# Attention heads by halves of the PE array, experts chosen by counting, a dummy pow, and scratch in a ring of 24 tiles

## The chip, the cores and the metric

The kernel runs on one core of a Trainium2 chip. The metric is the device time of one execution in microseconds (us), the median over several executions. The core has five engines with queues of their own: PE (matrix products; its weight loads are listed as PEld), DVE and ACT (element by element), POOL (rarely used here) and SP, which only issues transfers from DRAM.

## The reference

Two layers over 256 tokens of width 1024. Layer 0 mixes tokens with a gated convolution and stick-breaking attention, layer 1 with a gated MLP. Each layer then has a mixture of 32 experts (4 groups of 8; top group, then its top 2) and a gated embedding. All weights are float32, 257 MB in all.

```python
def even_mixer(xn, w_in, conv_w, w_out):
    proj = xn @ w_in
    ...
    y_a = short_conv_mixer(h, gb, gc, conv_w)
    y_b = stick_breaking_attention(q.reshape(shp), k.reshape(shp), v.reshape(shp))
    y = jnp.concatenate([y_a, y_b.reshape(B, S, SB_WIDTH)], axis=-1)
    return y @ w_out
...
def hier_moe(xn, wc, bc, wf, bf, w1, w3, w2):
    pc = jax.nn.softmax((xt @ wc + bc).astype(jnp.float32), axis=-1)
    pg, gi = lax.top_k(pc, 1)
    ...
    pf = jax.nn.softmax(lf_sel, axis=-1)
    wtop, ei = lax.top_k(pf, TOP_K)
    ...
    for e in range(N_EXPERTS):
        he = jax.nn.silu(xt @ w1[e]) * (xt @ w3[e])
        y = y + comb[:, e:e + 1] * (he @ w2[e])
```

## The kernel before

**Weights.** Nearly all weights come as tiles of 1 MB (128 partitions x 2048 float32), one transfer each, issued by SP in `emit_loads` (L109), in the order in which they are used. They land in a ring of 23 places (`rawp`, BUFS); a new tile takes the place that was released longest ago, and its transfer waits for the last user of that place. A tile of the dense stages is split into a high part `wh` (ACT, L126) and the rest `wl` (DVE, L136), each again a place of the ring, and each product is made of three (`mm3`). Expert tiles are used as they are. Some intermediate tensors (`att`, `xc`, `hT`, `o`) take places too; others have buffers of their own (`act`).

**How far ahead.** `emit_loads` goes on as long as `len(raws) + 2 * len(done) + 1 + SPARE + hold <= BUFS`, where `raws` are the tiles loaded and not yet split or used, `done` the split ones, SPARE is 4 and `hold` a number that each stage sets: HOLD[0] at the start, HOLD[1] after the attention, HOLD[3] when the odd mixer's output loop begins, HOLD[4] late in that loop, HOLD[2] after an expert stage, MOE_HOLD[0] (-2) in `finish_mixer`, which ends each mixer, and the other MOE_HOLDs inside the expert stage.

**Layer 0.** The input projection goes in column blocks (`proj_cols`, PE L411). For each of the two halves of the heads, `att_z` makes the scores z of two pairs of heads (a pair is 128 rows: head i in rows 64 i to 64 i + 63), then come softplus work on ACT and DVE and two or three projection blocks, `att_sum` (the running sum, PE L600 and L603) and `att_av` (the products with v, L612 and L613). `finish_mixer` makes the last output product, the router's logits (`lps`, L468) and 40 matmuls that have no use but to keep PE busy (L495).

**Expert stage.** The router (L786 to L820) picks the group by `first_max` and two experts in it by two more, each a chain of a maximum, an equality with a descending ramp `desc`, another maximum and another equality. The mask Mb goes to PE (L826), which counts positions; `gather` (L855) brings the tokens of a group together, and the 8 rounds q do `up` (hps, L907) with w1 and w3, and `down` (yps, L960) with w2; the 32-column quarters of the array each have another expert. The first users of the preloaded tiles are the first hps.

**The setup** has POOL make index ramps (jp first), from which DVE makes the identity and the masks; PE warms up for some us and transposes rows and x. `rstd` (POOL L370) is a power of -0.5.

**Layer 1** is as layer 0 with the gated MLP: `proj_u`, `gate`, and an output loop of 8 rounds.

## Time and profile before

| | us |
|---|---|
| median of 3 runs | 770.53 (766.19 to 770.72) |
| profiled execution | 771.92 |
| its span, first to last instruction | 770.1 |
| PE busy | 674.0 (88%) |
| DVE busy | 329.5 (43%) |
| ACT busy | 235.6 (31%) |
| POOL busy | 23.8 (3%) |
| bytes read from DRAM | 257.28 MB |

The mean granted clock of PE is 0.952 of full speed. In the program's order the stages are: layer 0's mixer up to about 131 us, its experts to 340, embedding and the mixer of layer 1 to 522, its experts to 731, the end. A window's row gives the busy time of each engine in a stretch with its count of instructions, then the granted clock, the share of the DMA engines and the GB/s. A timeline's row gives start, duration, engine, line, operation, result<-operands, partitions x elements, and the count when neighbours are drawn together; what stands in brackets is idle time before it and what ended that.

### The profile page before, as it was taken

How to read it: one execution, taken by the hardware profiler on the slowest of the kernel's cores; microseconds unless marked ns; L12 is line 12 of the kernel's file. 1: busy time of each engine (PE TensorE's matmuls, PEld its weight loads, DVE VectorE, ACT ScalarE, POOL GpSimd, SP SyncE). 2: the span in 40 equal slices, each digit the busy share in tenths (PEclk: the TensorE clock that was granted, in tenths of full speed). 3: DMA queues.
4: the chain of work that ended last, by engine and by line, in shares of the span. 5: the costliest groups of instructions: out<-in, count | busy, mean ns of one | idle time of the engine just before them, and what ended most of it. 6: DMA issues, size and time to landing. Idle time of an engine off the chain costs nothing.

```text
span 770.1 us, 12423 instructions
## 1 busy us (share of the span) xinstructions
PE 674.0 (88%) x5268; PEld 484.5 (63%) x5268; DVE 329.5 (43%) x556; ACT 235.6 (31%) x342; POOL 23.8 (3%) x36
## 2 busy tenths in 40 slices
PE   7999999889787797689999999998989868786696
PEld 6989988745353453237788999887554525443265
DVE  6546763332233031137765866644132421311266
ACT  6425644111101201127654443524101021010074
POOL 3200000000000000001100000000000000000000
PEclk9999999899998999999999999998999989898899
DMA  9950499699999999999854745398999999999941
GB/s 313 373 199 32 167 407 428 277 425 426 427 426 426 426 426 427 424 415 409 282 182 146 273 165 193 142 419 346 417 426 425 427 426 426 426 427 423 422 161 54
DMA packets 61163, 259.18 MB, mean 337 GB/s; under 512 B 4308, under 2 KB 22896, under 8 KB 36272
## 3 DMA queue, kind: packets, MB, share of 16 engines
q1 hardware_dynamic: 60032, 255.87, 82.5%
q0 software_dynamic: 1072, 2.47, 0.9%
q8 instruction: 43, 0.70, 0.3%
q14 instruction: 16, 0.13, 0.0%
HBM read 257.28 MB, written 1.05 MB: 335 GB/s over the span
## 4 chain that ended last, share of the span: by engine, by line
PE 47%; DMA 41%; DVE 6%; ACT 2%; issue 1%; POOL 1%; SPq 0%; POOLq 0%; ACTq 0%; DVEq 0%
DMA raw<-in_moe_w_dram 36%; PE pc L411 13%; PE ops L254 9%; PE pr L254 8%; PE hps L907 6%; PE gat L855 4%; DMA raw<-in_w_pe_dram 3%; PE yps L960 1%; DMA raw<-in_w_pg_dram 1%; DVE wl L133 1%; PE gps L712 1%; PE lps L468 1%; DVE wl L136 1%; DMA h<-in_x_dram 1%; PE tp L376 1%
## 5 line engine op out<-in xcount | busy, mean ns | idle before, releaser
L907 PE MATMUL hps<-raw,xg 128*32 128x256 f32 x2048 | 151.8, 423 | 41.0 <-DMA raw<-in_moe_w_dram 33.4
L907 PEld LDWEIGHTS hps<-raw,xg 128*32 128x32 f32 x2048 | 73.9, 121 | 117.2 <-DMA raw<-in_moe_w_dram 45.5
L136 DVE TENSOR_TENSOR wl<-raw,wh 128x2048 fp32r<-128x2048 f32 (+1 forms) x45 | 95.2, 2146 | 13.4 <-ACT wh L126 13.0
L960 PE MATMUL yps<-raw,gHL 128*32 128x512 f32 x512 | 62.4, 608 | 19.8 <-ACT gHL L947 17.8
L126 ACT CAST wh<-raw 128x2048 fp32r<-128x2048 f32 (+1 forms) x41 | 73.5, 1825 | 6.5 <-DMA raw<-in_w_in_even_dram 6.5
L928 ACT CAST ST<-sl 128x256 fp32r<-128x256 f32 x16 | 6.0, 372 | 217.2 <-DVE gjunk L924 215.2
L855 PE MATMUL gat<-S,xc 128*128 128x256 f32 (+1 forms) x320 | 64.6, 367 | 8.8 <-DVE S L841 8.8
L855 PEld LDWEIGHTS gat<-S,xc 128*128 128x128 f32 x320 | 56.3, 214 | 17.6 <-DVE S L841 9.7
L971 DVE SCALAR_TENSOR_TENSOR o<-yps,gts,o 128x512 fp32r<-128x512 f32 x28 | 21.0, 750 | 94.0 <-ACT o L970 94.0
L960 PEld LDWEIGHTS yps<-raw,gHL 128*32 128x32 f32 x512 | 15.7, 111 | 55.1 <-issue 30.0
L411 PE MATMUL pc<-xTH,wh 128*128 128x256 f32 x288 | 43.1, 296 | 1.2 <-DVE wh L128 1.2
L857 DVE TENSOR_TENSOR xg<-gat,gffn 128x512 f32<-128x512 f32 x32 | 22.1, 692 | 46.3 <-PE gat L855 42.6
L254 PE MATMUL pr<-wh,xTH 128*128 128x512 f32 (+1 forms) x152 | 40.6, 389 | 1.3 <-ACT xTH L388 1.3
L411 PEld LDWEIGHTS pc<-xTH,wh 128*128 128x128 f32 x288 | 39.7, 202 | 2.0 <-ACT xTH L521 1.4
L411 PE MATMUL pc<-xTL,wh 128*128 128x256 f32 x288 | 40.5, 284 | 0.0
L970 ACT ACTIVATE o<-yps,gts 128x512 fp32r<-128x512 f32 x28 | 19.2, 687 | 69.2 <-PE yps L960 49.7
L411 PE MATMUL pc<-xTH,wl 128*128 128x256 f32 x288 | 40.3, 283 | 0.0
L254 PE MATMUL pr<-wl,xTH 128*128 128x512 f32 (+1 forms) x152 | 39.5, 381 | 0.2 <-DVE wl L136 0.2
L254 PE MATMUL pr<-wh,xTL 128*128 128x512 f32 (+1 forms) x152 | 39.1, 379 | 0.0
L448 DVE TENSOR_TENSOR h<-h,sc 128x512 f32<-128x512 f32 x56 | 36.0, 683 | 7.0 <-PE sc L979 6.5
L938 DVE TENSOR_TENSOR he<-sl,hps 128x256 f32<-128x256 f32 x16 | 6.7, 421 | 72.0 <-PE hps L907 72.0
L411 PEld LDWEIGHTS pc<-xTL,wh 128*128 128x128 f32 x288 | 37.4, 194 | 0.0
(230 smaller groups left out, 867.9 us busy)
## 6 DMA issues: line engine op xcount, KB each, us to landing
raw<-in_moe_w_dram SPq DMA_DIRECT2D x192, 1024.0 KB, 19.5
raw<-in_w_in_odd_dram SPq DMA_DIRECT2D x16, 1024.0 KB, 13.2
raw<-in_w_in_even_dram SPq DMA_DIRECT2D x11, 1024.0 KB, 11.7
raw<-in_w_pg_dram SPq DMA_DIRECT2D x8, 1024.0 KB, 15.2
raw<-in_w_out_odd_dram SPq DMA_DIRECT2D x8, 1024.0 KB, 4.9
raw<-in_w_out_even_dram SPq DMA_DIRECT2D x4, 1024.0 KB, 5.0
raw<-in_w_pe_dram SPq DMA_DIRECT2D x2, 1024.0 KB, 19.5
h<-in_x_dram SPq DMA_DIRECT2D x2, 512.0 KB, 4.8
```

The source lines that it names most:

```text
L126: nc.scalar.copy(wh[:, c], raw[:, c])
L133: nc.vector.scalar_tensor_tensor(wl[:, c], raw[:, c], cols[:, col + j:col + j + 1], f(wh[:, c]), op0=ALU.mult, op1=ALU.subtract)
L136: nc.vector.tensor_tensor(wl[:, c], raw[:, c], f(wh[:, c]), op=ALU.subtract)
L254: nc.tensor.matmul(ps, x, w, start=start and i == 0, stop=stop and i == 3 * n - 1)
L411: nc.tensor.matmul(o, w, xx, start=st, stop=True if first else i % (3 * KD) == 3 * KD - 1, skip_group_check=first)
L448: nc.vector.tensor_tensor(h[:, tt, c], h[:, tt, c], ps, op=ALU.add)
L855: nc.tensor.matmul(ps[:, k], xc[:, tt, k0 + k, :], S[g][:, tt, c0:c1], start=(tt == 0), stop=(tt == 1))
L857: nc.vector.tensor_tensor(xg[g][:, k0:k0 + n, c0:c1], ps, gffn[:, li, k0:k0 + n].unsqueeze(2).to_broadcast([P, n, m]), op=ALU.mult)
L907: nc.tensor.matmul(ps[e * CAP:(e + 1) * CAP, :], x[:, k, c:c + CAP], ts[e][:, k, :], start=(k == 0), stop=(k == KD - 1))
L960: nc.tensor.matmul(ps[s, c], gs[:, j, s], ts[e][:, j, c], start=(j == 0), stop=(j == 1))
L970: nc.scalar.activation(o[:, 0, c], ps[:, c], AF.Copy, scale=gt[:, 0:1])
L971: nc.vector.scalar_tensor_tensor(o[:, 1, c], ps[:, c], gt[:, 0:1], f(o[:, 0, c]), op0=ALU.mult, op1=ALU.subtract)
```

## The change

The ring has 24 places; the holds are adjusted. The scratch tensors `u`, `gt`, `hs`, `zc`, `yH`/`yL` of the odd mixer, `xt`, `ptok` and `gts` move from buffers of their own into the ring (`carve` cuts one place into several views). In `att_z` the products of both heads of a pair stand next to each other and the masks follow; in `att_av` head i writes columns 64 i to 64 i + 63 of the array's output, so that one cast and one subtraction do for both. The router ranks the entries by counting those that are larger, and the maxima that the gates need are made after the first gather. A power of one is computed at POOL's head and not used.

```diff
-BUFS = 23
+BUFS = 24
 SPARE = 4
-HOLD = (9, 2, 8, 5, 3)
-MOE_HOLD = (-2, 2, 8, 4, -1)
+HOLD = (10, 2, 9, 9, 6)
+MOE_HOLD = (-2, 3, 8, 4, -1)
...
+    pone = small("pone", [P, 1])
+    nc.vector.memset(pone, 1.0)
+    nc.gpsimd.tensor_tensor(pone, pone, mhalf[:, 0:1], op=ALU.pow)
     jp = act("jp", [P, P])
...
         def att_z(hp):
             z = pp.tile([P, 2, 512], F32, name="z", tag="y")
+            rows = [slice(i * 64, (i + 1) * 64) for i in range(2)]
+
+            for i, rr in enumerate(rows):
+                nc.tensor.matmul(z[:, i, 0:256], qk[rr, 1, hp, 0:P], qk[rr, 0, hp, :], start=True,
+                                 stop=True)
+            for i, rr in enumerate(rows):
+                nc.tensor.matmul(z[:, i, 256:384], qk[rr, 1, hp, P:T], qk[rr, 0, hp, P:T],
+                                 start=False, stop=True, skip_group_check=True)
             for i in range(2):
...
+                for c in (0, 256):
+                    nc.tensor.matmul(z[:, i, c:c + P], ident_b, negmask, start=False, stop=True,
+                                     skip_group_check=True)
...
+            yb = psum("yb", "tp")[:, 0:T]
+
+            for tt, c in ((0, slice(0, T)), (1, slice(P, T))):
+                for i in range(2):
+                    vs = slice(hp * P + i * 64, hp * P + (i + 1) * 64)
+                    nc.tensor.matmul(yb[i * 64:(i + 1) * 64, c], v[:, tt, vs],
+                                     aT[:, i, c.start + 128 * tt:c.stop + 128 * tt],
+                                     start=(tt == 0), stop=True, skip_group_check=tt == 1)
+            nc.scalar.copy(yH[:, 4 + hp, :], yb)
+            nc.vector.tensor_tensor(yL[:, 4 + hp, :], yb, f(yH[:, 4 + hp, :]), op=ALU.subtract)
...
-            acc = act("hs", [P, 2, T])
...
-            hs = act("hs", [P, 2, T])
+            hs, zc, acc = [halves(a) for a in carve("conv", 2 * T, 2 * T + 4, 2 * T)]
...
-            u = act("u", [P, 2, T])
+            u, gt = [a.rearrange("p (c t) -> p c t", c=2) for a in carve("u", 2 * T, 2 * T)]
...
+        def rank_in(vals, n, tagp):
+
+            d = small(tagp + "d", [P, 2, n, n])
+            nc.vector.tensor_tensor(d, vals.unsqueeze(2).to_broadcast([P, 2, n, n]),
+                                    vals.unsqueeze(3).to_broadcast([P, 2, n, n]), op=ALU.subtract)
+            nc.vector.tensor_tensor(d, d, thr[:, 0:n, 0:n].unsqueeze(1).to_broadcast([P, 2, n, n]),
+                                    op=ALU.is_gt)
+            rk = small(tagp + "r", [P, 2, n])
+            nc.vector.tensor_reduce(rk, d, axis=AX.X, op=ALU.add)
+            return rk
```

On PE, the first scores of a pair of heads in layer 0, before (head 0, then head 1, of the first pair):

```order
L567 MATMUL z<-qk 128x256
L568 MATMUL z<-qk 128x128
L570 LDWEIGHTS ident_b
L570 MATMUL z<-negmask,ident_b 128x128
L572 LDWEIGHTS ident_b
L572 MATMUL z<-negmask,ident_b 128x128
L567 MATMUL z<-qk 128x256
L568 MATMUL z<-qk 128x128
```

and after the change:

```order
L576 MATMUL z<-qk 128x256 x2
L579 MATMUL z<-qk 128x128 x2
L583 LDWEIGHTS ident_b
L583 MATMUL z<-negmask,ident_b 128x128
L583 LDWEIGHTS ident_b
L583 MATMUL z<-negmask,ident_b 128x128
L583 LDWEIGHTS ident_b
L583 MATMUL z<-negmask,ident_b 128x128
L583 LDWEIGHTS ident_b
L583 MATMUL z<-negmask,ident_b 128x128
```

The two products of 64 rows with the same number of columns are neighbours now (x2: one per head), and the four mask products come in one block.

On DVE, the router of layer 0 from the logits lg to the mask Mb, before (c: group, f1 and f2: first and second expert):

```order
L804 SCALAR_TENSOR_TENSOR lg<-lps,rstd,br_231 128x36 x2
L786 TENSOR_REDUCE cm<-lg 128x2
L789 SCALAR_TENSOR_TENSOR ce<-lg,cm,desc 128x4 x2
L792 TENSOR_REDUCE cf<-ce 128x2
L794 TENSOR_TENSOR co<-ce,cf 128x8
L810 TENSOR_TENSOR pr<-lg,co 128x64
...
L792 TENSOR_REDUCE f2f<-f2e 128x2
L794 TENSOR_TENSOR f2o<-f2e,f2f 128x16
L818 TENSOR_TENSOR f1o<-f1o,f2o 128x16
L820 TENSOR_TENSOR Mb<-f1o,co 128x64
```

and after:

```order
L812 SCALAR_TENSOR_TENSOR lg<-lps,rstd,br_235 128x36 x2
L797 TENSOR_TENSOR cd<-lg 128x32
L799 TENSOR_TENSOR cd<-cd,thr 128x32
L802 TENSOR_REDUCE cr<-cd 128x8
L817 TENSOR_SCALAR G<-cr 128x8
L819 TENSOR_TENSOR pr<-lg,G 128x64
L822 TENSOR_REDUCE lsel<-pr 128x16
L797 TENSOR_TENSOR fd<-lsel 128x128
L799 TENSOR_TENSOR fd<-fd,thr 128x128
L802 TENSOR_REDUCE fr<-fd 128x16
L826 SCALAR_TENSOR_TENSOR Mb<-fr,G 128x32 x2
```

The chain from lg to Mb has 20 instructions behind the two of lg before, and 11 after.

On SP, the end of the transfers issued ahead of the expert stages. A tile's number counts all tiles of the program in the order in which they are made, so that a leap in it shows the code that stands between. MoE 0 before, then after:

```order
L109 DMA raw_1144<-in_moe_w2_dram 128x2048
L109 DMA raw_1146<-in_moe_w3_dram 128x2048
L109 DMA raw_1148<-in_moe_w3_dram 128x2048
L109 DMA raw_1150<-in_moe_w3_dram 128x2048
L109 DMA raw_1198<-in_moe_w3_dram 128x2048
L109 DMA raw_1200<-in_moe_w1_dram 128x2048
L109 DMA raw_1412<-in_moe_w1_dram 128x2048
```

```order
L113 DMA raw_1138<-in_moe_w3_dram 128x2048
L113 DMA raw_1140<-in_moe_w3_dram 128x2048
L113 DMA raw_1142<-in_moe_w3_dram 128x2048
L113 DMA raw_1144<-in_moe_w3_dram 128x2048
L113 DMA raw_1192<-in_moe_w1_dram 128x2048
L113 DMA raw_1194<-in_moe_w1_dram 128x2048
L113 DMA raw_1393<-in_moe_w1_dram 128x2048
```

Ahead of the leap of some 200 numbers one tile of the next round (w1) is issued before and two after. The first tiles of MoE 1, before and after:

```order
L109 DMA raw_3682<-in_w_out_odd_dram 128x2x1024
L109 DMA raw_3753<-in_moe_w1_dram 128x2048
L109 DMA raw_3783<-in_moe_w1_dram 128x2048
L109 DMA raw_3854<-in_moe_w1_dram 128x2048
L109 DMA raw_3884<-in_moe_w1_dram 128x2048
L109 DMA raw_3955<-in_moe_w3_dram 128x2048
L109 DMA raw_3985<-in_moe_w3_dram 128x2048
L109 DMA raw_4056<-in_moe_w3_dram 128x2048
L109 DMA raw_4086<-in_moe_w3_dram 128x2048
L109 DMA raw_4140<-in_moe_w1_dram 128x2048
L109 DMA raw_4142<-in_moe_w1_dram 128x2048
```

```order
L113 DMA raw_3815<-in_w_out_odd_dram 128x2x1024
L113 DMA raw_3845<-in_moe_w1_dram 128x2048
L113 DMA raw_3914<-in_moe_w1_dram 128x2048
L113 DMA raw_3944<-in_moe_w1_dram 128x2048
L113 DMA raw_4013<-in_moe_w1_dram 128x2048
L113 DMA raw_4043<-in_moe_w3_dram 128x2048
L113 DMA raw_4097<-in_moe_w3_dram 128x2048
L113 DMA raw_4099<-in_moe_w3_dram 128x2048
L113 DMA raw_4101<-in_moe_w3_dram 128x2048
```

Before, eight expert tiles are issued one by one between uses in the odd mixer and then two at once (4140, 4142); after, five one by one and then three at once (4097 to 4101).

## Rows read from the trace of the kernel before

**Rows 1.** Windows: attention, end of layer 1's mixer, MoE 1 (columns above).

```profile
50.70:103.60 52.90, 52.90 (x402) 50.27 (x401) 32.49 (x41) 31.42 (x36) 0.00 (x0) 1.00 0.38 142
420.00:515.00 95.00, 95.00 (x631) 87.30 (x630) 60.92 (x64) 38.43 (x34) 0.69 (x1) 1.00 0.63 231
545.00:725.00 180.00, 144.59 (x1353) 78.19 (x1353) 44.14 (x88) 21.48 (x43) 1.30 (x2) 0.92 1.01 426
```

**Rows 2.** Transfers 94:150: GB/s per 1.4 us; SP issues, us to landing.

```profile
GB/s 211 421 228 363 433 415 433 421 433 427 427 433 404 439 410 433 427 427 445 410 439 415 433 427 427 427 427 433 415 427 415 427 433 421 222 23 0 0 76 222
126.55 0.34 SPq L109 DMA_DIRECT2D raw<-in_moe_w_dram  x1
raw<-in_moe_w_dram SPq DMA_DIRECT2D x1, 1024.0 KB, 17.6
147.48 0.80 SPq L109 DMA_DIRECT2D raw<-in_moe_w_dram  x2
raw<-in_moe_w_dram SPq DMA_DIRECT2D x2, 1024.0 KB, 6.9
```

**Rows 3.** The same for 496:541 (1.125 us per slice), MoE 1.

```profile
GB/s 0 0 0 87 299 422 437 422 415 430 415 415 422 437 408 444 437 401 444 437 401 444 444 393 444 444 408 444 422 408 430 430 422 430 306 44 0 80 218 393
517.59 0.33 SPq L109 DMA_DIRECT2D raw<-in_moe_w_dram  x1
raw<-in_moe_w_dram SPq DMA_DIRECT2D x1, 1024.0 KB, 19.2
538.03 0.38 SPq L109 DMA_DIRECT2D raw<-in_moe_w_dram  x1
raw<-in_moe_w_dram SPq DMA_DIRECT2D x1, 1024.0 KB, 7.9
```

**Rows 4.** Timeline of PE: scores of one head, first row of the next.

```profile
50.74 0.70 PE L567 MATMUL z<-qk 64*128 64x256 f32 x2
51.28 0.38 PE L568 MATMUL z<-qk 64*128 64x128 f32 x2
51.59 0.23 PE L570 MATMUL z<-negmask,ident_b 128*128 128x128 bf16 x1
...
51.81 0.70 PE L567 MATMUL z<-qk 64*128 64x256 f32 x2
```

**Rows 5.** Timeline of PE: products with v, two neighbouring pairs of heads.

```profile
74.53 0.60 PE L612 MATMUL yb<-att,v 128*128 128x256 f32 x2
...
75.83 0.60 PE L612 MATMUL yb<-att,v 128*128 128x256 f32 x2
```

**Rows 6.** Timeline of PE: the first hps of MoE 0.

```profile
143.81 3.66 PE L907 MATMUL hps<-raw,xg 128*32 128x256 f32 x64
```

**Rows 7.** Timeline: router of MoE 0, logits to S.

```profile
131.37 0.42 DVE L804 SCALAR_TENSOR_TENSOR lg<-lps,rstd,br 128x36 f32<-128x36 f32 x2 [2.54 <-PE lps L468]
...
135.81 0.23 DVE L820 TENSOR_TENSOR Mb<-f1o,co 128x64 bf16<-128x64 f32 x1
136.09 0.18 PE L826 MATMUL rps<-Mb,upper_b 128*128 128x32 bf16 x1 [2.58 <-DVE Mb L820]
...
136.65 0.76 DVE L841 TENSOR_TENSOR S<-place,slots 128x256 f32<-128x256 f32 x2
```

**Rows 8.** The head, the first pow (timelines), and all pows of L370.

```profile
1.11 0.25 DVE L279 TENSOR_SCALAR ident<-jp 128x128 f32<-128x128 f32 x1
4.30 0.24 PE L325 MATMUL tpc<-ident,grows 8*128 8x8 f32 x1
15.88 4.49 DVE L136 TENSOR_TENSOR wl<-raw,wh 128x2048 fp32r<-128x2048 f32 x2
16.05 4.90 POOL L370 TENSOR_TENSOR rstd<-msq,mhalf 128x2 f32<-128x2 f32 x1 [11.14 <-DVE msq L369]
21.01 0.69 PE L361 MATMUL rb<-ident,rstd 128*128 128x128 f32 x2 [3.36 <-POOL rstd L370]
L370 POOL TENSOR_TENSOR rstd<-msq,mhalf x6: 688/713/4902, 16.1 to 745.7; 128x2 f32<-128x2 f32 x6
```

More of the change, by code (lines that the diff above doesn't have):

```diff
@@ L69, in big, with carve @@
         return rawp.tile(shape, dt, name=name, tag="raw")
-    act_tag = {"u": "wa", "sl": "wa", "ptok": "wa",
-               "gt": "wb", "he": "wb",
-               "hs": "wc", "yH": "wc", "gHL": "wc", "xt": "wc",
-               "rbc": "ST", "rows": "ST", "grows": "ST", "jp": "wb",
-               "zc": "wd", "yL": "wd", "S": "wd"}
+    act_tag = {"rbc": "ST", "rows": "ST", "grows": "ST", "jp": "S"}
+    def carve(name, *widths):
+        t, o, views = big(name, [P, 2048]), 0, []
+        for w in widths:
+            views.append(t[:, o:o + w])
+            o += w
+        return views
     def act(name, shape, dt=F32):
@@ L302, in body @@
     nc.vector.scalar_tensor_tensor(own, own, 0.0, low, op0=ALU.is_le, op1=ALU.mult)
-    desc = cp.tile([P, 2, 8], F32, name="desc")
-    nc.gpsimd.iota(desc, pattern=[[0, 2], [-1, 8]], base=8, channel_multiplier=0,
+    thr = cp.tile([P, 8, 8], F32, name="thr")
+    nc.gpsimd.iota(thr, pattern=[[-1, 8], [1, 8]], base=0, channel_multiplier=0,
                    allow_small_or_imprecise_dtypes=True)
+    nc.vector.tensor_scalar(thr, thr, 0.0, -1e-37, op0=ALU.is_lt, op1=ALU.mult)
     for c0, g in ((FFN_C, norm_ffn), (PL_C, norm_pl), (MIX_C, norm_mix[1:2, :])):
@@ L608, in att_av, with halves, conv @@
             aT = sps[hp]
-            yb = psum("yb", "tp").rearrange("p (i t) -> p i t", t=T)
-            for i in range(2):
-                vs = slice(hp * P, (hp + 1) * P)
-                nc.tensor.matmul(yb[:, i, :], v[:, 0, vs], aT[:, i, 0:256], start=True, stop=True)
-                nc.tensor.matmul(yb[:, i, 128:256], v[:, 1, vs], aT[:, i, 256:384], start=False,
-                                 stop=True, skip_group_check=True)
-            for i in range(2):
-                rr = slice(i * 64, (i + 1) * 64)
-                nc.scalar.copy(yH[rr, 4 + hp, :], yb[rr, i, :])
-                nc.vector.tensor_tensor(yL[rr, 4 + hp, :], yb[rr, i, :], f(yH[rr, 4 + hp, :]),
-                                        op=ALU.subtract)
-        def conv(gps, hs, i):
-            zc = act("zc", [P, 2, T + 2])
+            yb = psum("yb", "tp")[:, 0:T]
[7 more added lines that the diff above has]
+            nc.vector.tensor_tensor(yL[:, 4 + hp, :], yb, f(yH[:, 4 + hp, :]), op=ALU.subtract)
+        def halves(a):
+            return a.rearrange("p (c t) -> p c t", c=2)
+        def conv(gps, hs, zc, acc, i):
             nc.vector.memset(zc[:, :, 0:2], 0.0)
             nc.vector.tensor_tensor(zc[:, :, 2:T + 2], gps, hs, op=ALU.mult)
-            acc = act("hs", [P, 2, T])
             for c in range(2):
@@ L807, in moe @@
         lc = lg[:, :, 0:NG]
-        mc, G = first_max(lc, NG, "c")
+        G = small("G", [P, 2, NG])
+        nc.vector.tensor_scalar(G, rank_in(lc, NG, "c"), 0.5, None, op0=ALU.is_lt)
         pr = small("pr", [P, 2, NG, EPG])
@@ L813, in moe @@
         nc.vector.tensor_reduce(lsel, pr.rearrange("p a g e -> p a e g"), axis=AX.X, op=ALU.add)
-        m1, E1 = first_max(lsel, EPG, "f1")
-        l2 = small("l2", [P, 2, EPG])
-        nc.vector.scalar_tensor_tensor(l2, E1, NEG, lsel, op0=ALU.mult, op1=ALU.add)
-        m2, E2 = first_max(l2, EPG, "f2")
-        nc.vector.tensor_tensor(E1, E1, E2, op=ALU.add)
+        rk = rank_in(lsel, EPG, "f")
         Mb = small("Mb", [P, 2, NG, EPG], BF16)
-        nc.vector.tensor_tensor(Mb, *by_expert(E1, G), op=ALU.mult)
+        for tt in range(2):
+            nc.vector.scalar_tensor_tensor(Mb[:, tt], rk[:, tt].unsqueeze(1).to_broadcast([P, NG, EPG]),
+                                           1.5, G[:, tt].unsqueeze(2).to_broadcast([P, NG, EPG]),
+                                           op0=ALU.is_lt, op1=ALU.mult)
         Mf = Mb.rearrange("p a g e -> p a (g e)")
@@ L863, in moe @@
         gather(0, 4, 4, "y", 0, P)
+        mc, m1 = small("mc", [P, 2]), small("m1", [P, 2])
+        nc.vector.tensor_reduce(mc, lc, axis=AX.X, op=ALU.max)
+        nc.vector.tensor_reduce(m1, lsel, axis=AX.X, op=ALU.max)
         ec = small("ec", [P, 2, NG])
@@ L870, in moe @@
         nc.scalar.activation(small("warm", [P, 1]), mhalf[:, 0:1], AF.Silu)
-        nc.vector.tensor_tensor(lsel, lsel, E1, op=ALU.mult)
+        nc.vector.scalar_tensor_tensor(lsel, rk, 1.5, lsel, op0=ALU.is_lt, op1=ALU.mult)
         zf = small("zf", [P, 2])
@@ L1186, in per_layer @@
                 rows_part(pss[j], xH, xL, *ws[i], i, tt, slice(c0, c1))
[L1187 removed]
+        gts = carve("gts", 512, 256, 256)
+        sigmoid(pss[0], 0, gts[0])
+        sigmoid(pss[1], 1, gts[1])
         def scale(tt, c, act):
```

49 lines of the change are left out of this document (13 added, 36 removed).

## The prediction

> **What bounds the kernel now.** I read the windows by stage first, then the bytes per slice at the two entries into an expert stage, then single instructions.
>
> The stages have two different limits. In the attention of layer 0, PE is busy 52.90 of 52.90 us while DMA is at 0.38; in layer 1's mixer it is busy 95.00 of 95.00 with DMA at 0.63 [rows 1]. There only fewer or shorter matmuls help. In the expert stages DMA is at 1.01 of its engines and 426 GB/s, and PE has some 35 us of slack in 180 [rows 1]. A 1 MB tile (1.049 MB) then takes 2.44 us at the row's rate, and the stage ends when its last tile has landed. What counts there is how many tiles have landed when the stream starts to be continuous, and whether it has holes.
>
> Each expert stage has one hole, at its entry. Before MoE 0 the last tile loaded ahead is issued at 126.55 and lands 17.6 us later, at 144.2; the next ones are issued from 147.48, since they wait for the first up matmuls (hps) to free a tile, and the second of them (issued 147.90) lands 6.9 later, at 154.8 [rows 2]. One tile of 2.44 us lies between: DMA stands still for 154.8 − 2.44 − 2.44 − 144.2 = 5.8 us, and the row of GB/s shows it as two zeros at its end. Before MoE 1 the last tile ahead is issued at 517.59 and lands 19.2 later (536.8), the next pair's second is issued at 538.03 and lands at 545.9 [rows 3]: a hole of 545.9 − 4.88 − 536.8 = 4.2 us. In rows 3 the stream is continuous from the fourth slice (about 499) to there; before that DMA has slack.
>
> So layer 0's time is set by PE up to the first hps, from there by the stream; layer 1's by PE up to about 499, from there by the stream again.
>
> **A. Heads in halves.** Per pair of heads the scores take two rounds. One round is two passes of 256 columns (50.74 to 51.28, 0.54 us), two of 128 (to 51.59, 0.31) and two masks (to 51.81, 0.22), 1.07 together, 2.13 for both heads [rows 4]. The heads use different row halves. If two matmuls on different halves run side by side, a pair costs 0.54 + 0.31 + four masks, at most 2 × 0.22 = 0.44, together 1.29: a gain of 0.84, four times 3.4 us. The products with v take 1.31 per pair (74.53 to 75.83) [rows 5]; in column halves side by side one head's 0.65 remains, with 0.15 for what does not overlap: 0.51 less, four times 2.0. Sum **−5.4 us**, all on a PE without idle time. No row shows halves side by side. The nearest is the hps group, 64 passes of 256 columns over 32-column quarters in 3.66 us, 0.057 each [rows 6] against 0.22 and more for a pass above: quarters that are issued in turn do run together. That is why I take the overlap for columns and, less surely, for rows. Bounds: without overlap only changes between 64-row and 128-row products are saved, two per pair, each no longer than half of the two masks' 0.22: 4 × 0.2 = 0.8; with overlap and no leftover at 2.0's place 2.6, 6.0 in all. DVE and ACT also save instructions (one cast and one subtract per pair instead of two), off the path.
>
> The Trainium skill, TensorEngine Tiling (Array Packing), section Overview, says that the array works as independent tiles when the contraction or the output is 64 wide or less, up to twice as fast. By that rule the sum would be near the upper bound; here the quarters of hps agree, and no row shows halves.
>
> **C. Router.** Between the logits (DVE 131.37) and the chosen mask Mb (135.81 + 0.23) lie 4.67 us of small DVE operations that each need the one before [rows 7]: 22 instructions, 0.21 each with the step between them. PE waits 2.58 for the last. The changed chain has 13 (the order on DVE shows both): two for lg, three of counting for the groups, G, pr, lsel, three for the experts, two for Mb. 13 × 0.21 = 2.76. Three of them now handle 128 elements a partition, between Mb's 0.23 for 64 and S's 0.38 for 256 (0.76 for two) [rows 7], some 0.12 more each, and the step from one to the next is in full between nearly all of them: 3.1 to 3.3, of which I take the upper. Gain **−1.4 us** in MoE 0, where the first hps sets the stream; it is less than the wait of 2.58, so PE gets all of it (bounds: 0.8, with 0.3 for each of the 13, and 1.6). In MoE 1 it only moves the first hps, and there the stream decides: 0.
>
> **D. One tile more ahead of MoE 0.** The hold of −2 is unchanged, the ring has 24: 22 instead of 21 tiles ahead, as the order on SP shows. The tile is loaded inside the hole: **−2.44 us**. Does the hole hold it? The stream's start near 95 us comes earlier by the part of A before it (four z, two yb: 4.4; the other two yb stand behind it in the program), the first hps by A + C = 6.8. The hole is then 5.8 − 2.44 − (6.8 − 4.4) = 0.96 us, still open, so the three gains add up. But only 0.96 is left for more.
>
> **E. The ring in layer 1.** At the last holds of the odd mixer the limit on loaded tiles falls (16 to 14), and until then by three (14 to 11); SP's order shows five expert tiles ahead of the burst after the change for seven before it. From 499 on the stream is continuous, so two tiles more must come behind: 4.88 us, of which the hole takes 4.2: **+0.65** (0.4 to 1.5, since the slices of 1.1 us in rows 3 show the hole as 3.4 to 4.5). The odd mixer's own weights don't notice: DMA is at 0.63 there [rows 1], so they are loaded as soon as the ring has a place, and one place fewer delays each by one use; if it did come late, each such tile would cost up to 2.44.
>
> **B. Dummy pow.** The first pow starts at 16.05, takes 4.90 where the median is 0.713, and PE stops 3.36 us for its result [rows 8]. Two readings: a cost of the first use, which the dummy takes over, or DVE's two-operand subtractions (15.88 to 20.37) holding POOL back; the pow ends 0.58 after them. For the second speaks that end, for the first that the other five were short. I take **0** for the sum, and −3.4 (PE's stop) to −4.2 (what the pow took over the median) as the other end. If the dummy itself takes 4.9 us at the head, jp behind it is late, and DVE's ident ends at 1.11 + 0.25 + 4.9 = 6.3 where PE first uses it at 4.30 [rows 8]: at worst +2.0.
>
> **Scratch in the ring.** u, gt, hs, zc and the rest no longer have buffers of their own; tile addresses in the ring stay. A scratch tile now waits for the last user of the place that it gets, where it waited for its own predecessor of the same kind. In the PE-bound stage DVE is busy 60.92 of 95 us and ACT 38.43 [rows 1], so a write that starts a us later is covered: 0, with E holding what the places cost in loads; without that cover each late write would stop PE by what it is late.
>
> **Sum.** −5.4 − 1.4 − 2.44 + 0.65 = −8.59 us. The profiled execution spans 770.1 of 771.9 us; its span becomes 761.5 and its time 763.3. The median of the runs is 1.4 below the profiled one: 770.53 − 8.59 = **761.9**.
>
> **The rivals.** A measurement of this kernel tells about 1% from no change, 7.7 us; the bound lies at 762.8.
> - R1, row halves don't run side by side: A is 0.8 to 2.8, the sum −4.0 to −6.0; at the better end 764.5. For it: no row shows them; against it: hps's quarters.
> - R2, the pow pays: −3.4 more, 758.5 (down to 757.7); it lies ahead of the stream and shifts all behind it. The stop before PE's rb matmuls is gone and the dummy at the head takes some 4.9, of which up to 2.0 shows. For it: one pow in six is long, and it is the first. Against it: it ends just behind DVE's work. The Trainium skill, GPSIMD Engine Reference, section on instruction dispatch, puts about 6 us on the first call of a freshly loaded kernel; by that rule the 4.90 is such a load and R2 holds. The Trainium skill, SBUF — State Buffer, section SBUF: two separate sides, has a DVE instruction with two SBUF inputs lock POOL out for its length; by that rule the dummy brings nothing. Rows 8 agree with both.
> - R3, the lead into MoE 1: the fewer tiles held cost more than two. Each costs 2.44 beyond the 4.2 of the hole, so at six (14.6 − 4.2 = 10.4, against 9.2 won) the kernel is slower than before, 771.7; at nine by over 1%. The order shows two, and the stream's rate in rows 3 leaves no reason for more.
> - R4, part of the gain is given back at a release in the ring that opens late in MoE 0 (the 0.96 left is used up, a tile more or less): 2.44 to 5 us, 765.5.
>
> **How the numbers follow.** The forecast's case has 0.42, R1 0.15, R2 0.27, R3 0.07, R4 0.09. The forecast's own range is 760 to 764 (A from 4.5 to 6, C from 0.8 to 1.6, E from 0.4 to 1.5, and 0.96 of further gain that the hole leaves), about three fifths of it below 762.8. Faster by over 1%: 0.27 from R2, 0.26 from the forecast, 0.02 from R1: 0.55. Slower: R3's 0.07 at the most, of which part is within 1%: 0.06. The rest, 0.39, is within 1%. For 8 in 10 the range reaches from R2 with 4.2, the larger A and C, the smaller E and what the hole leaves then (756) to R4 and R1 with some of E's upper bound (767): R3 and the far end of R1 are left out.
>
> **What would show it.** A: z pairs 1.3 us and yb pairs 0.8 apart, attention about 5.5 shorter; if they stay at 2.1 and 1.3, R1. C: Mb at 3.3 after lg, PE's wait there about 1.2. D: the zeros in the GB/s row before MoE 0 shrink to one slice. E: no hole near 537, and the stream's last tile relative to the start of the continuous stretch 4.9 later. B: the first pow at 0.7 instead of 4.9, or not. The prediction fails if MoE 0's stream starts later than its first hps frees, or if a wait appears on ACT or DVE for a ring tile.

## The result and the profile after

The changed kernel takes 758.89 us in the median of its first 4 executions (758.14 to 761.62), against 770.62 of the kernel before: ratio 0.986, 95% interval 0.982 to 0.990. Measured once more later, beside the last experiments, it is 761.05 (6 executions) against 770.02, ratio 0.990 (0.987 to 0.993). So it is 1.0 to 1.4% faster; 761.9 was forecast. Its profiled execution took 761.62 and spans 759.8 us, 10.3 less than the one before.

Where the 10.3 us are, from the first start of an instruction of PE in each trace (us from the start of the span; pr: last projection ahead of the scores, ops: first output product, rps: first product with the router's mask, hps: first expert product, scl: the first product of an expert stage's last scatter, wps: filling matmuls of layer 1):

| from | to | before | after | difference |
|---|---|---|---|---|
| start | pr | 39.74 | 39.77 | +0.03 |
| pr | ops (attention) | 63.80 | 57.86 | -5.94 |
| ops | rps (to the router's mask) | 32.54 | 30.98 | -1.56 |
| rps | hps (gather) | 7.72 | 6.68 | -1.04 |
| hps | scl (MoE 0) | 199.63 | 196.99 | -2.64 |
| scl | wps (layer 1's mixer) | 178.87 | 178.54 | -0.33 |
| wps | scl (MoE 1) | 212.41 | 213.24 | +0.83 |
| scl | end | 35.4 | 35.7 | +0.4 |

The timeline of PE after the change, in the attention (start, duration, engine, line, operation, result<-operands, partitions, count), answers rows 4 and 5:

```profile
50.77 0.70 PE L576 MATMUL z<-qk 64*128 64x256 f32 x4
51.30 0.39 PE L579 MATMUL z<-qk 64*128 64x128 f32 x4
51.62 0.40 PE L583 MATMUL z<-negmask,ident_b 128*128 128x128 bf16 x4
51.95 0.70 PE L576 MATMUL z<-qk 64*128 64x256 f32 x4
...
72.74 1.52 PE L625 MATMUL yb<-att,v 128*64 128x256 f32 x16
74.19 0.70 PE L576 MATMUL z<-qk 64*128 64x256 f32 x4
```

Four passes of 64 rows and 256 columns (50.77 to 51.30) take the 0.53 us that two took in rows 4: the two row halves run side by side. A pair of heads is through in 51.95 - 50.77 = 1.18 (2.13 before), and two pairs of products with v in 74.19 - 72.74 = 1.45 (2.6 before).

The timeline from the router to the gather, which answers rows 7, has a chain of 3.15 us from lg to the end of Mb (4.67 before), and PE waits 0.97 for it instead of 2.58:

```profile
125.51 0.42 DVE L812 SCALAR_TENSOR_TENSOR lg<-lps,rstd,br 128x36 f32<-128x36 f32 x2 [2.54 <-PE lps L478]
...
127.40 0.29 DVE L797 TENSOR_TENSOR fd<-lsel 128x128 f32<-128x128 f32 x1
...
128.37 0.29 DVE L826 SCALAR_TENSOR_TENSOR Mb<-fr,G 128x32 bf16<-128x32 f32 x2
128.61 0.18 PE L834 MATMUL rps<-Mb,upper_b 128*128 128x32 bf16 x1 [0.97 <-DVE Mb L826]
...
129.81 5.55 PE L863 MATMUL gat<-S,xc 128*128 128x128 f32 x32 [0.86 <-DVE S L849]
135.29 1.07 PE L918 MATMUL hps<-raw,xg 128*32 128x256 f32 x16
```

The transfers into MoE 0 (GB/s per 1.25 us from 94 to 144, then SP's issues with the us to landing) answer rows 2:

```profile
GB/s 406 413 413 419 426 426 439 433 426 400 419 426 433 426 433 433 419 426 426 439 426 426 419 426 426 433 426 439 413 419 426 419 439 426 426 413 216 256 406 406
121.40 0.33 SPq L113 DMA_DIRECT2D raw<-in_moe_w_dram  x1
...
138.96 0.33 SPq L113 DMA_DIRECT2D raw<-in_moe_w_dram  x1
raw<-in_moe_w_dram SPq DMA_DIRECT2D x1, 1024.0 KB, 5.6
```

The 22nd tile is issued at 121.40, where before it had to wait for the first hps at 147.48. Two slices at half rate are left of the hole: 1.1 us. The slices of rows 2, counted in the same way, give 6.6 (5.8 by the landings). In the second profile of the changed kernel the gather was 1.6 us shorter, and the same window shows no hole at all:

```profile
GB/s 419 419 419 419 419 433 433 426 439 413 433 433 419 426 426 419 419 419 433 433 426 433 433 439 433 419 426 426 400 419 426 433 433 426 433 426 426 419 426 419
```

The row of GB/s into MoE 1 (1.4 us per slice from 484 to 540) answers rows 3. There the stream is continuous from about 490 on and has no hole:

```profile
GB/s 433 152 0 117 410 427 421 427 415 415 439 410 451 415 433 415 427 433 415 451 415 439 404 421 421 433 439 415 439 421 427 415 404 445 415 433 427 427 410 421
```

And the head, which answers rows 8. The dummy takes 0.55 us at the head, and the first real pow takes 4.91 as before; DVE's two subtractions stand beside it again:

```profile
1.14 0.55 POOL L282 TENSOR_TENSOR pone<-pone,mhalf 128x1 f32<-128x1 f32 x1 [0.69 <-DVE pone L281]
...
4.19 0.25 PE L335 MATMUL tpc<-ident,grows 8*128 8x8 f32 x1
...
15.60 4.49 DVE L140 TENSOR_TENSOR wl<-raw,wh 128x2048 fp32r<-128x2048 f32 x2
15.77 4.91 POOL L380 TENSOR_TENSOR rstd<-msq,mhalf 128x2 f32<-128x2 f32 x1 [10.05 <-DVE msq L379]
...
20.74 0.43 PE L371 MATMUL rb<-ident,rstd 128*128 128x128 f32 x2 [2.73 <-POOL rstd L380]
```

### The profile page after: what moved, and what is told of

Its sections match the earlier page's. It is cut to its first block, busy times and chain, and to the rows that moved or that the text cites. A ratio compares the mean times of both kernels' runs of the same rounds, so it can differ in the third digit from the quotient of the medians.

```text
span 759.8 us, 12425 instructions
## 1 busy us (share of the span) xinstructions
PE 661.5 (87%) x5268; PEld 475.3 (63%) x5268; DVE 325.6 (43%) x540; ACT 233.8 (31%) x338; POOL 24.4 (3%) x37
## 4 chain that ended last, share of the span: by engine, by line
PE 47%; DMA 41%; DVE 6%; ACT 3%; issue 1%; POOL 1%; SPq 0%; POOLq 0%; ACTq 0%; DVEq 0%
DMA raw<-in_moe_w_dram 36%; PE pc L421 13%; PE ops L258 9%; PE pr L258 8%; PE hps L918 6%; PE gat L863 3%; DMA raw<-in_w_pe_dram 3%; PE yps L971 2%; DMA raw<-in_w_pg_dram 1%; DVE wl L137 1%; PE gps L724 1%; DMA raw<-in_w_in_even_dram 1%; PE lps L478 1%; DVE wl L140 1%; ACT wh L128 1%
## 5 line engine op out<-in xcount | busy, mean ns | idle before, releaser
L863 PE MATMUL gat<-S,xc 128*128 128x256 f32 (+1 forms) x320 | 61.8, 356 | 8.8 <-DVE S L849 8.8
L863 PEld LDWEIGHTS gat<-S,xc 128*128 128x128 f32 x320 | 54.0, 205 | 17.1 <-DVE S L849 9.7
```

Source lines behind the costliest of these rows:

```text
L863: nc.tensor.matmul(ps[:, k], xc[:, tt, k0 + k, :], S[g][:, tt, c0:c1], start=(tt == 0), stop=(tt == 1))
```

## The experiments

The kernels were timed in three groups, each beside the kernel before. Medians in us, and within the profiled execution of each the stretches of the table above that the arguments need ("pow" is the first real pow):

| kernel | median | ratio (95%) | pow | start to pr | attention | gather to hps | MoE 0 | MoE 1 |
|---|---|---|---|---|---|---|---|---|
| before | 770.6 | 1 | 4.90 | 39.74 | 63.80 | 6.58 | 199.63 | 212.41 |
| after | 758.9 | 0.986 (0.982 to 0.990) | 4.91 | 39.77 | 57.86 | 5.48 | 196.99 | 213.24 |
| after, again | 761.1 | 0.990 (0.987 to 0.993) | 4.91 | 39.72 | 57.86 | 3.85 | 197.31 | 213.54 |
| before, halves only | 762.3 | 0.991 (0.988 to 0.994) | 2.70 | 35.07 | 57.86 | 6.29 | 199.46 | 212.65 |
| before, counting only | 767.4 | 0.997 (0.995 to 0.999) | 2.70 | 36.21 | 63.79 | 3.85 | 202.11 | 213.44 |
| after, hold for 21 tiles | 761.0 | 0.990 (0.987 to 0.993) | 2.71 | 36.41 | 57.86 | 3.85 | 198.46 | 213.30 |
| after, ring of 23 | 763.2 | 0.991 (0.989 to 0.994) | 2.71 | 35.34 | 57.86 | 3.85 | 199.51 | 213.67 |
| after, more lead | 756.1 | 0.985 (0.980 to 0.989) | 2.71 | 35.43 | 57.86 | 3.85 | 197.40 | 208.92 |
| after, rb later | 759.6 | 0.987 (0.983 to 0.992) | 4.91 | 35.96 | 57.86 | 3.85 | 198.28 | 213.32 |
| after, 56 filling matmuls | 760.3 | 0.987 (0.982 to 0.992) | 4.91 | 39.32 | 57.86 | 3.85 | 197.65 | 213.19 |
| after, 24 pows more (one execution) | 762.7 | - | 4.91 | 40.71 | 57.86 | 5.48 | 197.16 | 213.31 |
| after, no dummy | 761.0 | 0.989 (0.986 to 0.992) | 4.90 | 39.02 | 57.86 | 5.48 | 197.24 | 213.37 |
| three changes | 754.0 | 0.979 (0.977 to 0.982) | 4.92 | 37.04 | 57.86 | 3.85 | 199.01 | 209.88 |
| three changes, one tile more | 751.4 | 0.977 (0.974 to 0.980) | 4.91 | 36.81 | 57.86 | 3.86 | 198.19 | 208.86 |

The attention's stretch repeats far better than the medians: it takes 57.86 in all twelve rows of this table that have the halves. The head does not repeat. Where PE's order in it is that of before and POOL has no more pows, it lies between 35.07 and 39.77, and the column of the pow says most of the reason: counted from the start of the pow (14.77 to 16.10), pr comes 20.3 us later where the pow takes 2.7, and 23.7 to 24.0 later where it takes 4.9. A single time of one kernel therefore carries 3.3 us and more of chance, and arguments below go by stretches. MoE 0's stretch is no constant either. The stream sets its end, so it also depends on how far the stream has come at the first hps: with 24 places and the gather at 3.85 it lies between 197.31 and 199.01.

**Halves only.**

```diff
 # before, with att_z and att_av of the changed kernel
+            for i, rr in enumerate(rows):
+                nc.tensor.matmul(z[:, i, 0:256], qk[rr, 1, hp, 0:P], qk[rr, 0, hp, :], start=True,
...
+            yb = psum("yb", "tp")[:, 0:T]
...
```

> The kernel before with only the new att_z and att_av. The theory: halves of the array run side by side, rows as well as columns, so a pair of heads takes 1.2 us for its scores (2.13 before) and 0.73 for its products with v (1.31 before), and everything behind the attention, the first hps and so the whole stream of MoE 0 comes about 6 us earlier: time 764.5, ratio 0.992. Rival (only the number of changes between 64-row and 128-row products counts): 2.0 and 1.2 us, time 769 to 770. If the stream's start and not the first hps set MoE 0, the gain would be smaller than what the attention wins.

The attention is 5.94 us shorter, exactly as in the changed kernel, and the stretches behind it are those of before (MoE 0 199.46 for 199.63): the gain arrives whole at the end. The profiled execution spans 759.5 us, 10.6 less than before: 5.94 from the attention and 4.67 from the head, where the pow took 2.70. The median is 8.3 us lower (ratio 0.991), of which a part is the pow. The rival that only changes of form count is out.

**Counting only.**

```diff
 # before, with rank_in, thr and the later maxima of the changed kernel
-        mc, G = first_max(lc, NG, "c")
+        G = small("G", [P, 2, NG])
+        nc.vector.tensor_scalar(G, rank_in(lc, NG, "c"), 0.5, None, op0=ALU.is_lt)
...
```

> The kernel before with only the router that counts. The theory: from lg to Mb 3.1 us instead of 4.7, PE's wait for Mb about 1.0 instead of 2.6, and, since the stop is shorter, PE spends less of the gather at the lower clock (5.5 us instead of 6.65): first hps 2.6 us earlier, time 768, ratio 0.9965. Rival: the clock falls all the same and the gather stays at 6.65, then 1.6 us. In MoE 1 the first hps comes earlier too, but the stream's hole there must shrink by as much and no more than that is won: up to 1.6 us further, as the hole of 4.2 us there is open in this kernel.

The ratio 0.997 is the expected one, the way to it is not. The gather takes 3.9 us, less than the 5.5 expected, and PE's wait for Mb, expected at 1.0, is not there at all. The clock was at the lower level before the mask, while PE was busy; the 40 filling matmuls took 3.74 us instead of 2.40 and filled the wait, and in the gather the clock was up again. The timeline of PE and the windows of that kernel (busy us and count of PE, PEld, DVE, ACT, POOL, then clock, DMA share, GB/s) show this, and that the transfers run slower in this execution:

```profile
127.84 3.74 PE L496 MATMUL wps<-ones_b 128*128 128x128 bf16 x40
131.42 0.18 PE L824 MATMUL rps<-Mb,upper_b 128*128 128x32 bf16 x1
...
128.00:130.00 2.00, 2.00 (x22) 2.00 (x20) 1.65 (x8) 1.63 (x1) 0.00 (x0) 0.50 1.04 434
132.50:136.40 3.90, 3.84 (x32) 3.72 (x32) 0.94 (x2) 0.00 (x0) 0.00 (x0) 1.00 0.98 410
160.00:330.00 170.00, 134.59 (x1204) 72.06 (x1196) 42.49 (x83) 19.13 (x39) 0.75 (x1) 0.91 1.01 420
```

The same windows of the kernel before:

```profile
137.20:143.80 6.60, 6.58 (x32) 6.49 (x32) 0.91 (x2) 0.00 (x0) 0.00 (x0) 0.55 0.79 334
160.00:330.00 170.00, 133.55 (x1221) 71.45 (x1219) 43.46 (x87) 21.48 (x43) 0.75 (x1) 0.94 1.01 426
```

420 instead of 426 GB/s is 1.4%, or 2.8 us over an expert stage of 200 us; that accounts for MoE 0's 202.11 against 199.63. The further gain expected in MoE 1 did not show either (213.44 for 212.41); its transfers ran at 420 too. So the stretch to the router's mask is 1.1 us shorter here and 1.6 in the changed kernel, and from the mask to the first hps another 1.0 to 2.7 are won, by whether the clock is down in the gather; the slower transfers hid part of it here.

**Is it the 22nd tile? First try, by the hold.**

```diff
-MOE_HOLD = (-2, 3, 8, 4, -1)
+MOE_HOLD = (-1, 3, 8, 4, -1)
```

> The changed kernel with 21 instead of 22 tiles loaded ahead of MoE 0 and MoE 1 (MOE_HOLD[0] = -1). The theory: in MoE 0 the hole grows from 1.2 to 3.6 us and the stage ends 2.44 us later; in MoE 1 the stream has no hole, the tile is issued a little later but still in time: 0. Time 2.4 us longer than the changed kernel, about 761.3. Rival (the tile ahead is worth nothing, because the first hps comes so much earlier that its tiles are free in time): 0.

A miss: this did not undo what it was meant to undo. SP's row in this kernel:

```profile
121.70 0.33 SPq L113 DMA_DIRECT2D raw<-in_moe_w_dram  x1
```

The 22nd tile is issued at 121.70 all the same, long before the first hps. The median of 761.0 agrees with the 761.3 expected by luck, since what was to cost 2.4 us was not in place. The hold sets where in the program the transfer is written, but SP runs down its own queue and stops only at a place that is still in use; with 24 places this one was free.

**Second try, by the ring.**

```diff
-BUFS = 24
+BUFS = 23
-HOLD = (10, 2, 9, 9, 6)
-MOE_HOLD = (-2, 3, 8, 4, -1)
+HOLD = (9, 2, 8, 8, 5)
+MOE_HOLD = (-2, 2, 8, 4, -1)
```

> The changed kernel with 23 places in the ring and the holds lowered by one (one tile fewer ahead of the expert stages, the same number of expert tiles at the burst ahead of MoE 1). The theory: the 22nd tile ahead of MoE 0 now waits for the first hps; the hole at the entry of MoE 0 is 2.44 us longer than with 24 places, and the kernel is 2.4 us slower than the changed kernel in executions of the same kind. In the kernel with 21 tiles by the hold alone that tile was issued at 121.7 without waiting, because its place was free. Rival: the places of the scratch tiles, not the tile ahead, are what 24 is needed for: then waits on DVE or ACT appear in the odd mixer.

Now SP waits. Its waits from 117 to 134 (us in total, times, longest):

```profile
SPq L113 <- PE hps L918: 14.3, 1, 14.3
```

and MoE 0 takes 199.51. In the kernel with more lead, which has 24 places, the same gather and the head that agrees best (pr 35.43 for 35.34), it takes 197.40: 2.1 us for the place. Over all seven profiles with 24 places and that gather (197.31 to 199.01) it is 0.5 to 2.2. It does not come as the longer hole that was expected; of the hole one slice at 264 is there, 0.4 us (GB/s per 1.15 us from 94 to 140):

```profile
GB/s 413 435 435 420 420 435 413 420 427 427 435 420 427 427 435 420 427 427 435 420 427 427 435 427 420 427 427 413 427 420 435 427 427 420 420 264 420 427 413 413
```

Most of the loss lies ahead of it. Up to the first hps (129.23) 38.08 MB had been moved; with 24 places and more lead it was 38.87 MB (to 129.32), some 1.8 us of the stream. So the place also lets the loads run further ahead before the expert stage. The median is 763.2 against 758.9 and 761.1. The mixer of layer 1 takes 178.88 against 178.50 to 178.69, so the scratch loses at most 0.2 to 0.4 us without the 24th place.

**The lead into MoE 1.**

```diff
-HOLD = (10, 2, 9, 9, 6)
+HOLD = (10, 2, 9, 6, 4)
```

> The changed kernel with lower holds in the odd mixer (HOLD[3] 9 to 6, HOLD[4] 6 to 4), so that seven expert tiles instead of five have been issued at the burst ahead of MoE 1. The theory: in the changed kernel the stream into MoE 1 has no hole, so its length sets the stage; two tiles fewer behind it are worth up to 2 x 2.44 = 4.88 us, less what a new hole takes (first hps free at 524.5, the last tile ahead lands then at about 528.4, so a hole of 0 to 0.5): 4.4 to 4.9 us faster than the changed kernel, about 754.3. Rival: the places taken by expert tiles make the odd mixer's weights late, PE stops there, and the gain is eaten up: 0 or slower.

MoE 1 takes 208.92 instead of 213.24: 4.3 us, where 4.4 to 4.9 were expected, and the mixer ahead of it is unchanged (178.59). The median of 756.1 is above the 754.3 expected, with executions from 751.5 to 758.2. SP's issues in this kernel, with the us to landing:

```profile
501.00 0.33 SPq L113 DMA_DIRECT2D raw<-in_moe_w_dram  x1
raw<-in_moe_w_dram SPq DMA_DIRECT2D x1, 1024.0 KB, 19.7
...
519.03 0.33 SPq L113 DMA_DIRECT2D raw<-in_moe_w_dram  x1
raw<-in_moe_w_dram SPq DMA_DIRECT2D x1, 1024.0 KB, 6.7
```

From 520.7 to 525.7 two tiles land: 5.0 us for 4.88, so the hole is 0.1. The higher holds of the change cost what they take from the lead, and nothing in layer 1 needs them. They cost 0.83 against the kernel before and yet give 4.3 when lowered, because that kernel's hole of 4.2 has been paid for otherwise. The 24th place loads one tile more (2.44), and the first hps comes 1.6 us sooner behind the first filling matmul (10.05 us for 11.63); of 4.2 that leaves 0.2, an estimate close to the 0.1 found. By this estimate the router and the 24th place win time in MoE 1 too, and the holds of the change hid it.

**What the pow waits for.**

```diff
         r = norm.rstd()
+        px = small("px", [P, 24])
+        nc.gpsimd.memset(px, 1.0)
+        for j in range(24):
+            nc.gpsimd.tensor_tensor(px[:, j:j + 1], px[:, j:j + 1], mhalf[:, 0:1], op=ALU.pow)
         late_loads()
```

> The changed kernel with 24 pows more of one element per partition on POOL right behind the first real pow, beside DVE's subtractions of the setup; their results are not used. The theory of the port: a pow alone takes about 0.55 us; one that meets a subtraction of DVE with two operands from SBUF takes until that subtraction ends and 0.5 more, so that durations come in steps of 2.25 us and the ends follow those of DVE. The rival (first use of the code): all 24 take 0.55, whatever DVE does. POOL's transfers behind them come later, which costs nothing by the time the router needs them.

All 24, and single ones of them beside DVE (the first row: minimum, median, maximum in ns):

```profile
L549 POOL TENSOR_TENSOR px<-px,mhalf x24: 545/584/2607, 21.0 to 38.4; 128x1 f32<-128x1 f32 x24
22.72 2.28 DVE L140 TENSOR_TENSOR wl<-raw,wh 128x2048 fp32r<-128x2048 f32 x1
23.05 2.36 POOL L549 TENSOR_TENSOR px<-px,mhalf 128x1 f32<-128x1 f32 x1
...
26.88 0.58 POOL L549 TENSOR_TENSOR px<-px,mhalf 128x1 f32<-128x1 f32 x1
...
35.76 2.28 DVE L140 TENSOR_TENSOR wl<-raw,wh 128x2048 fp32r<-128x2048 f32 x1
36.02 2.43 POOL L549 TENSOR_TENSOR px<-px,mhalf 128x1 f32<-128x1 f32 x1
```

The pow that starts 0.33 us into a subtraction ends at 25.41, 0.41 behind DVE's 25.00; the one at 36.02 ends at 38.45, again 0.41 behind DVE's 38.04. A third, from 30.41 to 33.02, does the same behind the subtraction from 30.33 to 32.61. Two that were already running when a subtraction began (from 22.54 and 35.51) took 0.57 and 0.61. Where DVE does nothing, at 26.88, a pow takes 0.58. The code has been in use by then in all cases, so the first use is not what costs. The first real pow of the kernels, with either head, is 2.70 to 2.71 us in five profiles and 4.90 to 4.92 in nine: it waits for the running subtraction, and then for the next one too or not. What decides between the two no run shows. In all nine long cases and four of the short ones the two subtractions stand back to back (with counting only, DVE paused 0.39 us between them), and the kernel before (4.90) and the one with the halves only (2.70) have the same instructions up to there. So I call it a draw; but the one program that was profiled twice, the changed kernel, took 4.91 both times. In the traces it is worth 3.3 us at pr (36.41 in the kernel with the hold for 21 tiles against 39.72 in the changed kernel's second profile, whose starts agree), more than the 2.2 of one subtraction. The windows (columns as above) say why. The changed kernel's second profile, with 4.91:

```profile
18.00:20.00 2.00, 0.00 (x0) 0.00 (x0) 2.00 (x2) 1.31 (x1) 2.00 (x1) 1.00 1.07 414
20.00:22.00 2.00, 1.02 (x5) 1.02 (x6) 0.77 (x3) 1.27 (x2) 1.85 (x2) 0.57 1.02 384
22.00:24.00 2.00, 2.00 (x12) 2.00 (x12) 1.97 (x3) 1.34 (x2) 0.00 (x0) 0.57 1.08 389
```

and the kernel with the hold for 21 tiles, with 2.71:

```profile
18.00:20.00 2.00, 1.53 (x14) 1.35 (x14) 2.00 (x2) 1.21 (x2) 1.73 (x2) 1.00 1.06 410
20.00:22.00 2.00, 2.00 (x19) 2.00 (x18) 1.97 (x5) 1.31 (x2) 0.00 (x0) 1.00 1.05 393
```

After the long stop PE runs mostly at the 1.2 GHz level for some 3.5 us, after the short one it stays at 2.4. That holds for all six profiles in which PE stopped 2.7 us or more for the pow, and for all five in which it stopped 1.6 or less.

**The kernel without the dummy.**

```diff
-    pone = small("pone", [P, 1])
-    nc.vector.memset(pone, 1.0)
-    nc.gpsimd.tensor_tensor(pone, pone, mhalf[:, 0:1], op=ALU.pow)
```

> The changed kernel without the dummy pow at the head. The theory: the dummy brings nothing, since the first real pow waits for DVE and not for its code: the same time as the changed kernel within the spread, and the first real pow again at 2.7 or 4.9 us. The rival (first use): the first real pow takes longer than with the dummy, beyond one or two subtractions, and the time is 3 to 4 us longer.

761.01 against 761.05 of the changed kernel on the same chip, and 4.90 for its first real pow. The dummy brings nothing and costs nothing. **The changed kernel again**, beside it:

> The changed kernel itself, once more, for its size beside the three that follow: 759 to 761, ratio 0.985 to 0.988. Its executions should fall into two groups about 3.4 us apart, by whether the first pow waits for one or for two subtractions of DVE.

Its six executions run from 759.77 to 763.40 without two clear groups, and the median and ratio lie just above what was expected. The two groups did not show, and why is open. The kernel before does have two groups: of its 45 timed executions ten lie between 765.5 and 767.4, one at 768.2 and 34 from 769.1 to 772.5. That would fit the draw, but no trace of the lower group was kept.

**PE's stop for the pow, taken away.**

```diff
         make_cols(cols, rows, NCOL)
+        ps2 = proj_cols(xH, xL)
         rb = norm.rows()
...
-        ps = proj_cols(xH, xL)
```

> The changed kernel with the second projection of layer 0 issued on PE ahead of the transposes (rb) that need the first pow. In the traces the first pow takes 2.7 or 4.9 us, and it ends 0.58 us after the first or the second of two subtractions of DVE. The theory: POOL waits for DVE's running subtraction, by chance for one or for two of them; PE then stops 0.5 to 3.4 us. With other work ahead of rb the stop is gone in every execution: the projection's next block (pr) starts at about 35 us (39.8 and 36.4 in executions of the changed kernel), 1 to 4.7 us earlier, and the median is 2 to 4 us under the changed kernel's, with less spread. Rival: the second projection needs a split that DVE makes late as well, so PE waits there for DVE and nothing is won.

The pow drew 4.91 in this execution, and pr still starts at 35.96, as in the executions that drew 2.7. PE's waits from 10 to 40 (us in total, times, longest) no longer name POOL:

```profile
PE pc L421 <- DVE wh L132: 2.2, 1, 2.2
PE pc L421 <- DVE qk L552: 1.3, 1, 1.3
```

The second row is new: both projections wait in PE's accumulators for rb, and the third must wait for DVE to read one. The median of 759.6 shows no gain over the changed kernel, less than expected; the profiled one alone (757.5, its span 3.1 us less than that of the changed kernel's second profile) does. The four executions (757.5 to 760.2) leave it open why.

**The clock at the gather.**

```diff
-GAP_WARM = 40
+GAP_WARM = 56
```

> The changed kernel with 56 instead of 40 matmuls that fill PE's wait for the router (16 x 0.06 = 0.96 us, the wait was 0.97). The theory: without the stop PE stays at the 2.4 GHz level in every execution and the gather takes 3.9 us instead of 5.55; the first hps comes 1.6 us earlier, of which the hole of MoE 0 takes 1.2: up to 1.2 us faster than the changed kernel where the clock fell, 0 where it did not. Rival: the clock falls because of the second wait (0.86 us for S), then nothing changes.

The stop for Mb is gone, and the gather takes 3.9 us:

```profile
124.80 3.29 PE L505 MATMUL wps<-ones_b 128*128 128x128 bf16 x56
128.17 0.18 PE L834 MATMUL rps<-Mb,upper_b 128*128 128x32 bf16 x1
...
129.37 3.92 PE L863 MATMUL gat<-S,xc 128*128 128x128 f32 x32 [0.86 <-DVE S L849]
```

But so it does in five profiles that stop for 1.0 us, the changed kernel's second among them. In three (the changed kernel's first, without the dummy, and with 24 pows) it takes 5.5. So after stops of this length both happened, and one profile with more filling matmuls can't say that they are what kept the clock. The second wait of 0.86 for S alone did not bring it down in the gather in any of the four profiles without a stop for Mb. But a stop isn't needed either: in layer 1 of this same kernel the clock was down in the filling matmuls, with PE busy all the time,

```profile
506.80:509.50 2.70, 2.70 (x26) 2.70 (x25) 0.16 (x1) 2.62 (x5) 0.69 (x1) 0.96 1.01 428
509.50:512.50 3.00, 3.00 (x30) 3.00 (x30) 2.35 (x11) 2.98 (x3) 0.00 (x0) 0.50 1.01 426
```

as it was in layer 0 of the kernel with counting only. That the shorter stop is what keeps the clock up in the gather is therefore argued, not shown. In the time nothing shows: 760.3.

**The three changes together**, and with one expert tile more:

```diff
-HOLD = (10, 2, 9, 9, 6)
+HOLD = (10, 2, 9, 6, 4)      # then (10, 2, 9, 5, 3)
-GAP_WARM = 40
+GAP_WARM = 56
...
+        ps2 = proj_cols(xH, xL)
```

> The changed kernel with the three changes that the runs point to: the lower holds of the odd mixer (6 and 4), the second projection ahead of rb, and 56 filling matmuls. The theory: 4.2 us from the lead into MoE 1 (measured within one trace), up to 3.4 from the pow in the executions where it waited twice, up to 1.2 at the hole of MoE 0: 752 to 754 where the changed kernel takes 759 to 760. Rival: the stream of MoE 0 hides all that comes ahead of it, then only the 4.2: 755.

> As the kernel with the three changes, with one more expert tile ahead of the burst before MoE 1 (holds 5 and 3). The theory: with the lead of before the stream's hole at MoE 1 was 0.2 us, the filling matmuls make the first hps there 1.6 us earlier, so of the tile's 2.44 us 1.6 to 1.8 are won and a hole of some 0.8 stays: 750.5 to 752.5. Rival: the hole grows by all of 2.44 and nothing is won, because the first hps does not come earlier.

754.03 (ratio 0.979, at the upper end of what was expected) and 751.35 (0.977, interval 0.974 to 0.980). The second is 7.5 to 9.7 us faster than the changed kernel's two medians. MoE 1 takes 209.88 and 208.86, so most of it is the lead; MoE 0 with 199.01 and 198.19 gives back 1 to 2 us of what the earlier hps wins, since its hole is closed and the stream sets it.

## Why the prediction was right, step by step

**The total.** 761.9 forecast, 758.9 and 761.1 measured, both inside 756 to 767. On the profiled execution the sum said -8.6 and the trace says -10.3. The likeliest case held, with its terms in place. The 1.7 us more are the clock at the gather (1.0), A (0.5), and C and D (0.2 each), less 0.2 in layer 1 and the end. The first median of 758.9 lies outside the 760 to 764 that this case was given, and next to R2's 758.5; that nearness is luck, since R2's cause is not there: the head of the profile is unchanged (39.77 for 39.74). It is 2.7 under the profiled execution, where 1.4 had been taken over from the kernel before.

**A, -5.4 forecast, -5.94 measured.** The mechanism is the one forecast, near its upper bound of 6.0. A pair's scores cost 1.18 instead of 1.29: four masks take 0.33, less than twice 0.22. The products with v cost 0.73 a pair instead of 0.80. R1, row halves one after the other, is refuted by four passes in the time of two. The Trainium skill's rule of up to twice as fast (TensorEngine Tiling (Array Packing), Overview) is borne out for the products themselves: 0.53 for four as for two.

**C, -1.4 forecast, -1.56 measured**, and PE's wait came out at 0.97 for 2.58. The 128-element steps cost 0.29, within the bounds taken. What the sum left out is the clock: the gather now runs at the lower level for less of its time (5.48 us for 6.58), or not at all (3.85). It could pay only within the 0.96 that the forecast left open in the hole; it was 1.0 of the gain in the changed kernel's first profile. For MoE 1 the forecast gave C nothing, as the stream decides there; with more lead it seems to pay there too (the estimate under the lead into MoE 1).

**D, -2.44 forecast, -2.64 measured** over MoE 0, 2.1 by the ring of 23 against the profile that matches it best. The hole's remainder was forecast at 0.96 and is 1.1 in the first profile and nothing in the second. Two things were not forecast: not the hold but the free place lets the tile go, as the first try showed, and with 23 places most of the loss came ahead of the hole, not in it.

**E, +0.65 forecast, +0.83 measured** (+1.1 in the second profile), within 0.4 to 1.5. The hole at MoE 1 is gone, as forecast. The prediction reads five tiles for seven ahead of the burst; the order on SP shows five and then three for eight and then two, so eight for ten, and the difference of two that the sum uses stands. R3 did not happen.

**B, 0 forecast, 0 measured.** R2, with a chance of 0.27, is refuted twice: the dummy at the head took 0.55 us, and the first real pow behind it 4.91. The other reading was right, that POOL waits for DVE. The sign that the prediction named for it, 4.9 again, came. By the Trainium skill's SBUF — State Buffer, SBUF: two separate sides, a DVE instruction with two SBUF inputs locks POOL out. The three of the 24 pows that started behind such an instruction agree, each ending 0.41 us after it. The load of about 6 us that the Trainium skill, GPSIMD Engine Reference, section on instruction dispatch, puts on a first call appears in no run here. What the prediction missed is that it can be one subtraction or two, 3.3 us of the head, before and after the change alike; what decides it stays open. The forecast's "slow" end for the head (ident late by 2.0) didn't come either, PE's first use of it stands at 4.19 for 4.30.

**Scratch in the ring, 0 forecast, -0.33 measured** in layer 1's mixer. PE's waits in that mixer are those of before (1.3 us for ACT and 0.2 for DVE at its start), and with 23 places it was 178.88. No run tries the scratch alone, or the pad that the change also shortens (ALIGN, 256 to 64). R4 didn't happen: from 160 to 330 the transfers ran at 425 GB/s for 426 before, and MoE 0 is 2.64 shorter.

## What to carry to other kernels

Sum the parts stage by stage, with the stage's own limit: PE's savings in front of a saturated stream count as long as the stream has a hole to give, and a saving that a closed hole hides in one stage can pay once the loads run further ahead. Test a ring's lead in both directions, since the holds that the change raised were worth 4.3 us when lowered. Products over 64 rows or 64 columns pay at once when their partner half is issued right behind them, and before a cost is put down to a first use, compare its end with the ends of the neighbouring engine.
